# Mixer of a hybrid decoder trunk: products by V grouped by branch, weight splits queued behind a projection's first reader

## The chip, the cores and the metric

The kernel runs on one core of one Trainium2 chip, as one launch. The metric is the device time of that launch in microseconds (us), lower is better. A time of a kernel is the median of its runs; the profile is one further execution, with its own time.

## The reference, cut to what matters

Two layers, each of three sub-layers: a SwiGLU feed-forward block, a token mixer, a second feed-forward block. Sequence 256, width 1024, everything in float32. The change lies in the mixer alone:

```python
def _hybrid_mixer(u, w_in, b_gate, b_forget, w_branch, w_out):
    proj = u @ w_in
    a_qkv, b_qkv, i_q, i_k, i_w, c_qkv, d_qkv, f_logit, g_logit = jnp.split(proj, SPLIT_POINTS, axis=-1)
    ...                                     # A: 3 groups of 2 heads, dilated windows, rope, merged by softmax of lse
    y_b = _dsa_attention(qb, kb, vb, q_idx, k_idx, i_w).reshape(bsz, t, -1)      # 4 heads, rope, top 64 keys
    y_c = _stick_breaking_attention(qc, kc, vc).reshape(bsz, t, -1)              # 4 heads
    y_d = _forgetting_attention(qd, kd, vd, log_f).reshape(bsz, t, -1)           # 4 heads
    gates = jax.nn.sigmoid((g_logit + b_gate)...).reshape(bsz, t, N_BRANCH, D_MODEL)
    merged = gates[:, :, 0] * (y_a @ w_branch[...])
    for i in range(1, N_BRANCH):
        merged = merged + gates[:, :, i] * (branches[i] @ w_branch[...])
    return merged @ w_out
```

Every attention ends in a product of its weights p (256 x 256, causal) by V (256 x 64 a head).

## The kernel before

**Split products.** A product of float32 matrices runs as three matmuls on rounded halves: each operand is split into `hi` and `lo`, and `split_mm` (L289 to L295) adds hi by hi, hi by lo and lo by hi into a PSUM bank. The activations are split once per sub-layer (`uh`, `ul`). The weights are split as they arrive, in `load`: a DMA on SP's queue brings 128 x 1024 values into a `raw` tile (L261; five `raw` buffers, `RB`), ScalarE (ACT) rounds it to `hi` (L264), VectorE (DVE) subtracts to get `lo` (L270). A `raw` buffer is free for the next DMA when its `lo` is done. The reductions of the conditioning weights (L321, on DVE, from `adac`) take their `raw` buffers from the same five, in the same SP queue.

**Projections.** `proj` makes two blocks of 128 output channels into one PSUM bank from `mm_bank`, of which there are two. So projection n fills the bank that projection n-2 used, and waits until that one's readers are done. The readers are `rope` (DVE: L706 and L707 read the bank, then a shuffle, L708) for branches A, B and the indexer, and `plain` (ACT: L715) for C and D. The order in the program is: V of A (L1042), three projections of A (`qa`, `ka`), indexer `iq`, a `vproj` with the indexer's key, its weights and V of B and half of C, then `qb`, `kb`, `cq`, `ck`, a second `vproj` (V of C and D; its weights are 128 x 768 pieces, `mv`), `dq`, `dk`. Sixteen projections for the gates follow, with the branch products between them.

**Attention between the projections.** `plan` puts steps of the four attentions at numbered turns (`on`), which `tick` calls between projections. `a_scores`, `a_pt` and `a_pv` do branch A in two halves of 128 queries: scores, softmax (`soft`: minima on DVE L818, exponentials on ACT L820, reciprocal L821, scaling on ACT L824), transposes on TensorE (PE, L926) into a PSUM bank from `tp_bank`, of which there are two, a copy on ACT (L928) into a `pt` tile, products by V (L934). For C, D and B, `pair_pt` transposes two heads, `pair_pv` multiplies two heads by V (`pv`, L791 and L794) into a bank, and `y_out` rounds the 128 x 256 result to `yh` (ACT, L807) and `yl` (DVE, L808). Branch products (`tp<-y`) read these.

**What sets the order.** A scheduler orders each engine's instructions when the kernel is built, by program order and by priorities (`tc.high_priority(offset=...)` moves a block forward: `HP` for `load`, `RP` and `PP` for the readers, `VP` for V and y). Each engine then runs its list strictly in that order. `tc.issue_after(i)` puts what is traced inside it behind instruction i in that list, where both are on the same engine; it adds no wait between engines.

Of the kernel before, what the change touches and what calls it, by code (L numbers as in the profile page):

```python
# [18 lines left out]
D = 1024  # L19
# [44 lines left out]
GD = 3  # L64
PTB = 3
AST = 7
# [80 lines left out]
def trunk(ctx: ExitStack, tc: tile.TileContext, x, xT, crow, ada0, adac, adab, w_in0, w_in0x, gcol, bcol, ln_g, ln_b,  # L147
# [101 lines left out]

    def load(*srcs):  # L250

# [3 lines left out]
        for o in range(2):  # L255
            for src, n, half, got in zip(srcs, widths, halves, parts):
                if o * half >= n:
                    continue
                with tc.high_priority(offset=HP):
                    raw = wp.tile([P, 1024], F32, tag="raw", bufs=RB, name="raw")  # L260
                    nc.sync.dma_start(raw[:, :half], src[:, o * half:(o + 1) * half])  # L261
                    hi, lo = w_pair()
                    with behind() if held["free"] <= 0 < held["left"] else ExitStack():
                        nc.scalar.copy(hi[:, :half], raw[:, :half])  # L264
                        if held.get("pool_lo"):
                            held["pool_lo"] -= 1
                            nc.gpsimd.tensor_sub(lo[:, :half], raw[:, :half], hi[:, :half].bitcast(F32))
                        else:
                            with held["late"].pop(0) if held["late"] else ExitStack():
                                held["lo"] = nc.vector.tensor_sub(lo[:, :half], raw[:, :half], hi[:, :half].bitcast(F32)).ins  # L270
                    held["left"] -= 1
                    held["free"] -= 1
                    got.append((hi, lo))
# [394 lines left out]
    def mixer(l, u, nxt, steps):  # L668
# [15 lines left out]
        def tick():  # L684
            at["n"] += 1
            for f in turns.pop(at["n"], []):
                f()

        def proj(src, n):
            w = load(src.rearrange("p a b -> p (a b)"))  # L690
            ps = mm_bank()
# [9 lines left out]
        def rope(ps, name, scale=1.0):  # L701
# [3 lines left out]
            with tc.high_priority(offset=RP):  # L705
                nc.vector.scalar_tensor_tensor(t2, ps, scale, cs[:, C_SIN:C_SIN + 256], op0=ALU.mult, op1=ALU.mult)  # L706
                nc.vector.scalar_tensor_tensor(q, ps, scale, cs[:, C_COS:C_COS + 256], op0=ALU.mult, op1=ALU.mult)  # L707
            nc.vector.stream_shuffle(t3, t2, shuf)  # L708
            nc.gpsimd.tensor_tensor(q, q, t3, op=ALU.add)
            return q  # L710

        def plain(ps, scale, name):
            q = mp.tile([P, T], F32, tag="qk", bufs=QB, name=name)
            with tc.high_priority(offset=PP):
                nc.scalar.activation(q, ps, AF.Copy, scale=scale)  # L715
            return q

# [4 lines left out]
        def index_keys():  # L722
            ps = tp_bank()
            for t in range(2):
                nc.tensor.transpose(ps[:, t * 128:(t + 1) * 128], ik2[:, t].rearrange("p a b -> p (a b)"), ident)
            ik.append(rope(ps[:, :256], "ik"))

        wf = mp.tile([P, 2, 8], F32, tag="wf", bufs=1, name="wf")

        def vproj(srcs, width, piece, extra=0):  # L730
# [16 lines left out]
            else:  # L747
                for hf in range(2):
                    w = load(srcs[hf].rearrange("p a b -> p (a b)"))
                    for t in range(2):  # L750
# [46 lines left out]

        def y_out(y, k, t=None):

            c = slice(0, T) if t is None else slice(t * 128, t * 128 + 128)  # L800
            with tc.high_priority(offset=VP):
                if k in (0, 1, 3, 5) and not t:
                    ys["tile"] = alt([P, 4, T], F32R, "y")
                o = 2 * (k in (2, 4, 6))
                ys[k] = (ys["tile"][:, o], ys["tile"][:, o + 1])
                yh, yl = (z[:, c] for z in ys[k])
                nc.scalar.copy(yh, y)  # L807
# [83 lines left out]

        def pair_pv(br, j, k):
            y = acc_bank()
            pv(y, {h % 2: [(vh(br, h, 0), vh(br, h, 1), live.pop((br, h)))] for h in (2 * j, 2 * j + 1)})
            y_out(y[:, :T], k + j)

# [109 lines left out]
        def plan():  # L1006
# [15 lines left out]
            for j in range(2):  # L1022
                on(20 + CS + j, f(c_sums, j))
            for j in range(2):
                on(23 + CVV + j, f(pair_pv, "C", j, 3))
                on(26 + 6 * j, f(d_scores, j))
                on(38 + 6 * j, f(b_scores, j))
                on(29 + 6 * j, f(pair_pt, "D", j))
                on(30 + 6 * j, f(pair_pv, "D", j, 5))
                on(41 + 6 * j, f(pair_pt, "B", j))  # L1030
                on(42 + 6 * j, f(pair_pv, "B", j, 1))
            for n, t in enumerate(STEPS):
# [9 lines left out]
        vproj([mv12[l, 0, 0], mv12[l, 0, 1]], 384, 2)  # L1042
        qa, ka = [], []
        for i in range(3):
            for j, p in enumerate(proj(mpair[l, i], 2)):
                (qa if 2 * i + j < 3 else ka).append(rope(p, "qa", -0.125) if 2 * i + j < 3 else rope(p, "ka"))
        at["n"] = 0
        plan()
        iq = [rope(p, "iq") for p in proj(mpair[l, 3], 2)]
        vproj([mv0[l, 0], mv0[l, 1]], 456, 0, extra=72)  # L1050
        qb = [rope(p, "qb", -0.125) for p in proj(mpair[l, 4], 2)]
        kb = [rope(p, "kb") for p in proj(mpair[l, 5], 2)]
        cq = [plain(p, 0.125, "cq") for p in proj(mpair[l, 6], 2)]
        ck = [plain(p, 1.0, "ck") for p in proj(mpair[l, 7], 2)]
        vproj([mv12[l, 1, 0], mv12[l, 1, 1]], 384, 1)
        dq = [plain(p, -0.125, "dq") for p in proj(mpair[l, 8], 2)]
        dk = [plain(p, 1.0, "dk") for p in proj(mpair[l, 9], 2)]

# [166 lines left out]
```

## Time and profile before

| | |
|---|---|
| median of 3 runs | 1297.29 us (1295.61 to 1297.9) |
| the profiled execution | 1298.93 us, its span from first to last instruction 1297.1 us |
| PE busy | 1263.4 us, 97% |
| DVE busy | 1040.6 us, 80% |
| ACT busy | 655.5 us, 51% |
| granted PE clock, mean | 0.997 of full speed |
| mixers in the span | about 210 to 455 us and 850 to 1090 us |

The span is cut by what PE does, instruction after instruction. A matmul's own length in the timeline (0.28 us for 256 columns) is modelled and overlaps its neighbours; what it costs is the distance from its start to the next start, 0.12 us for 256 columns in a stream. So the places where PE waits show as wider steps between starts, with the releaser in brackets where one is known.

### The profile page before, as it was taken

Reading aid. Unit: us, or ns where it says so; the run is one execution under the profiler, and the core shown is the slowest. Engines: PE = TensorE matmul, PEld = TensorE weight load, DVE = VectorE, ACT = ScalarE, POOL = GpSimd, SP = SyncE. Lnnn points to the kernel's source line nnn. Section 1 sums busy time; section 2 is a strip of 40 time slices with the busy share of each in tenths; the row PEclk is TensorE's granted clock in tenths of the full one; section 3 lists DMA queues with packets and bytes.
Section 4 is the critical chain, followed back from the end, with each engine's and each line's share of the span. In section 5 each row is a group of like instructions: output and inputs, shape, how many; then the busy total and the mean of one; then the engine's idle time right before and its main releaser. Section 6 shows DMA issues by size and latency. Waiting matters only on the chain.

```text
span 1297.1 us, 23364 instructions
## 1 busy us (share of the span) xinstructions
PE 1263.4 (97%) x9178; PEld 1175.5 (91%) x9178; DVE 1040.6 (80%) x1701; ACT 655.5 (51%) x1023; POOL 144.6 (11%) x150
## 2 busy tenths in 40 slices
PE   6999999999999999999999999999999999999997
PEld 5989998999999889999989999898999997899995
DVE  7788987889796789986689976688989867896565
ACT  4563445447664465444364444454766554644440
POOL 0021000204131000000000000021071310000000
PEclk9999999999999999999999999999999999999999
DMA  9889963757775568975659875356577645765530
GB/s 341 332 280 361 375 241 131 240 177 235 241 253 195 206 235 309 327 256 191 211 191 316 322 255 179 118 184 216 195 245 248 236 168 199 275 236 185 194 132 33
DMA packets 85846, 300.41 MB, mean 232 GB/s; under 512 B 10604, under 2 KB 12316, under 8 KB 85736
## 3 DMA queue, kind: packets, MB, share of 16 engines
q1 hardware_dynamic: 84392, 298.00, 65.9%
q8 instruction: 72, 1.18, 0.3%
q10 hardware_dynamic: 576, 0.60, 0.1%
q0 software_dynamic: 768, 0.32, 0.1%
q14 instruction: 38, 0.31, 0.1%
HBM read 297.81 MB, written 1.07 MB: 230 GB/s over the span
## 4 chain that ended last, share of the span: by engine, by line
PE 76%; issue 8%; DVE 6%; DMA 5%; ACT 4%; POOL 1%; DVEq 0%; POOLq 0%; ACTq 0%; SPq 0%
PE mm L289 15%; PE mm L290 15%; PE mm L291 15%; PE acc L295 7%; PE acc L294 6%; PE acc L293 6%; ACT hi L264 2%; DVE lo L270 2%; PE tp L289 1%; DMA raw<-in_w_in_dram 1%; PE tp L290 1%; PE tp L291 1%; DMA raw<-in_w_out_dram 1%; DMA raw<-in_mpair_dram 1%; PE mm L293 1%
## 5 line engine op out<-in xcount | busy, mean ns | idle before, releaser
L270 DVE TENSOR_TENSOR lo<-raw,hi 128x1024 fp32r<-128x1024 f32 (+2 forms) x421 | 508.6, 1224 | 172.7 <-ACT hi L264 171.3
L264 ACT CAST hi<-raw 128x1024 fp32r<-128x1024 f32 (+1 forms) x422 | 434.7, 1041 | 367.4 <-PE mm L290 206.0
L289 PE MATMUL mm<-uh,hi 128*128 128x256 f32 x2032 | 574.4, 283 | 1.8 <-DVE qa L707 1.8
L290 PE MATMUL mm<-ul,hi 128*128 128x256 f32 x2032 | 571.3, 281 | 0.0
L291 PE MATMUL mm<-uh,lo 128*128 128x256 f32 x2032 | 570.5, 281 | 0.0
L289 PEld LDWEIGHTS mm<-uh,hi 128*128 128x128 f32 x2032 | 383.1, 189 | 8.2 <-issue 4.1
L290 PEld LDWEIGHTS mm<-ul,hi 128*128 128x128 f32 x2032 | 383.5, 189 | 1.4
L291 PEld LDWEIGHTS mm<-uh,lo 128*128 128x128 f32 x2032 | 383.3, 189 | 0.3
L295 PE MATMUL acc<-hi,hl 128*128 128x512 f32 x352 | 138.3, 398 | 4.0 <-DVE hl L558 3.8
L293 PE MATMUL acc<-hi,hh 128*128 128x512 f32 x352 | 140.2, 398 | 0.4 <-ACT hh L557 0.4
L294 PE MATMUL acc<-lo,hh 128*128 128x512 f32 x352 | 139.0, 395 | 0.0
L321 DVE CUSTOM_DVE_ANT_0 adac<-adac,cond_row,adab 128x1024 f32<-128x1024 f32 x80 | 101.8, 1284 | 3.0 <-DMA adac<-in_adac_dram 3.0
L295 PEld LDWEIGHTS acc<-hi,hl 128*128 128x128 f32 x352 | 65.7, 187 | 22.6 <-DVE hl L558 6.6
L293 PEld LDWEIGHTS acc<-hi,hh 128*128 128x128 f32 x352 | 66.1, 188 | 15.1 <-ACT hh L557 1.2
L294 PEld LDWEIGHTS acc<-lo,hh 128*128 128x128 f32 x352 | 66.1, 188 | 13.8
L557 ACT CAST hh<-h 128x256 fp32r<-128x256 f32 x82 | 33.2, 405 | 82.1 <-DVE h L551 82.1
L321 DVE CUSTOM_DVE_ANT_0 raw<-raw,cond_row,adab 128x1024 f32<-128x1024 f32 x48 | 66.9, 1408 | 0.0
L434 POOL TENSOR_TENSOR rstd<-rstd,nhalf 128x1 f32<-128x1 f32 x12 | 7.6, 634 | 475.1 <-DVE rstd L433 475.1
L558 DVE TENSOR_TENSOR hl<-h,hh 128x256 fp32r<-128x256 f32 x74 | 31.3, 423 | 12.6 <-ACT hh L557 12.6
L1102 POOL TENSOR_TENSOR merged<-merged,tg 128x512 f32<-128x512 f32 x16 | 28.0, 1752 | 120.2 <-DVE tg L1100 57.7
L293 PE MATMUL acc<-hi,uh 128*128 128x256 f32 (+1 forms) x128 | 38.8, 303 | 0.8 <-ACT uh L462 0.8
L295 PE MATMUL acc<-hi,ul 128*128 128x256 f32 (+1 forms) x128 | 38.1, 298 | 0.0
(243 smaller groups left out, 1551.7 us busy)
## 6 DMA issues: line engine op xcount, KB each, us to landing
raw<-in_w_in_dram SPq DMA_DIRECT2D x174, 512.0 KB, 5.5
raw<-in_mpair_dram SPq DMA_DIRECT2D x104, 512.0 KB, 4.7
raw<-in_w_out_dram SPq DMA_DIRECT2D x88, 512.0 KB, 5.2
adac<-in_adac_dram SPq DMA_DIRECT2D x80, 512.0 KB, 6.9
raw<-in_adac_dram SPq DMA_DIRECT2D x48, 512.0 KB, 4.5
ada<-in_ada_dram SPq DMA_DIRECT2D x16, 512.0 KB, 6.7
raw<-in_mwo_dram SPq DMA_DIRECT2D x16, 512.0 KB, 4.4
raw<-in_mv_dram SPq DMA_DIRECT2D x16, 384.0 KB, 3.6
```

What stands on the lines that cost most here:

```text
L264: nc.scalar.copy(hi[:, :half], raw[:, :half])
L270: held["lo"] = nc.vector.tensor_sub(lo[:, :half], raw[:, :half], hi[:, :half].bitcast(F32)).ins
L289: nc.tensor.matmul(ps, lhsT=wh, rhs=xh, start=start, stop=False)
L290: nc.tensor.matmul(ps, lhsT=wh, rhs=xl, start=False, stop=False)
L291: nc.tensor.matmul(ps, lhsT=wl, rhs=xh, start=False, stop=stop)
L293: nc.tensor.matmul(ps, lhsT=xh, rhs=wh, start=start, stop=False)
L294: nc.tensor.matmul(ps, lhsT=xh, rhs=wl, start=False, stop=False)
L295: return nc.tensor.matmul(ps, lhsT=xl, rhs=wh, start=False, stop=stop).ins
L321: nc.vector.tensor_tensor_reduce(raw, raw, cond_row, 0.5, adab_sb[:, l * 3 + s, v, n:n + 1], ALU.mult, ALU.add, accum_out=t[:, n:n + 1])
L557: nc.scalar.copy(hh, h)
L558: eng.tensor_sub(hl, h, hh.bitcast(F32))
L1102: eng.tensor_tensor(mg, mg, t, op=ALU.add)
```

## The change

Three things change, all in the mixer.

1. `pair_pv` (two heads) becomes `branch_pv` (four heads): both pairs' products by V go into the two halves of one PSUM bank, and one ACT copy and one DVE subtraction of 512 columns make `yh` and `yl` of the whole branch. It is called at one turn per branch (28 for C, 36 for D, 48 for B) where `pair_pv` was called at 27 and 28, 30 and 36, 42 and 48. `PTB`, the number of `pt` buffers, goes from 3 to 4.
2. `load` takes a list `after`; the split of the weights (L264, L270) is queued behind these instructions. `proj` and the `vproj` passes give it `readers[-2:-1]`: the first reader (L707, or L715 where the projection is `plain`) of the projection two back, the one whose bank they wait for.
3. Readers are recorded by `pair`, and forgotten after each `vproj`.

```diff
-PTB = 3
+PTB = 4
@@ load
-    def load(*srcs):
+    def load(*srcs, after=()):
...
-                    with behind() if held["free"] <= 0 < held["left"] else ExitStack():
+                    with behind() if held["free"] <= 0 < held["left"] else ExitStack() as order:
+                        for i in after:
+                            order.enter_context(tc.issue_after(i))
                         nc.scalar.copy(hi[:, :half], raw[:, :half])
@@ mixer
+        readers = []
         def proj(src, n):
-            w = load(src.rearrange("p a b -> p (a b)"))
+            w = load(src.rearrange("p a b -> p (a b)"), after=readers[-2:-1])
...
@@ vproj
-                    w = load(srcs[hf].rearrange("p a b -> p (a b)"))
+                    w = load(srcs[hf].rearrange("p a b -> p (a b)"), after=readers[-2:-1])
@@ y_out: A alone, a tile of its own
-                if k in (0, 1, 3, 5) and not t:
-                    ys["tile"] = alt([P, 4, T], F32R, "y")
+                if t == 0:
+                    ys["tile"] = alt([P, 2, T], F32R, "y")
@@
-        def pair_pv(br, j, k):
+        def branch_pv(br, k):
             y = acc_bank()
-            pv(y, {h % 2: [(vh(br, h, 0), vh(br, h, 1), live.pop((br, h)))] for h in (2 * j, 2 * j + 1)})
-            y_out(y[:, :T], k + j)
+            for j in range(2):
+                pv(y[:, j * T:(j + 1) * T], {h % 2: [(vh(br, h, 0), vh(br, h, 1), live.pop((br, h)))] for h in (2 * j, 2 * j + 1)})
+            with tc.high_priority(offset=VP):
+                both = alt([P, 2, 2, T], F32R, "y")
+                for j in range(2):
+                    ys[k + j] = (both[:, 0, j], both[:, 1, j])
+                yh, yl = (both[:, n].rearrange("p a b -> p (a b)") for n in range(2))
+                nc.scalar.copy(yh, y)
+            nc.vector.tensor_sub(yl, y, yh.bitcast(F32))
@@ plan
+            on(24 + CVV, f(branch_pv, "C", 3))
+            on(36, f(branch_pv, "D", 5))
+            on(48, f(branch_pv, "B", 1))
             for j in range(2):
-                on(23 + CVV + j, f(pair_pv, "C", j, 3))
...
-                on(30 + 6 * j, f(pair_pv, "D", j, 5))
...
-                on(42 + 6 * j, f(pair_pv, "B", j, 1))
@@ the projections
+        def pair(i, *makes):
+            got = [make(p) for make, p in zip(makes, proj(mpair[l, i], 2))]
+            readers.append(got[0][1])
+            return [q for q, _ in got]
...
+        qka = pair(0, aq, aq) + pair(1, aq, ak) + pair(2, ak, ak)
...
+        iq = pair(3, *[roped("iq")] * 2)
         vproj([mv0[l, 0], mv0[l, 1]], 456, 0, extra=72)
+        readers.clear()
+        qb = pair(4, *[roped("qb", -0.125)] * 2)
+        kb = pair(5, *[roped("kb")] * 2)
+        cq = pair(6, *[copied("cq", 0.125)] * 2)
+        ck = pair(7, *[copied("ck", 1.0)] * 2)
         vproj([mv12[l, 1, 0], mv12[l, 1, 1]], 384, 1)
+        readers.clear()
```

The changed kernel's line numbers run ahead: L264 of before is L266, L270 L272, L706 and L707 L712 and L713, L708 L714, L715 L721, L820 L825, L824 L829, L852 L857, L928 L941, L791 and L794 L797 and L800. Outside the two mixers, the order on every engine is as it was; SP's order of DMAs is the same throughout.

The first projections of A, on DVE (`lo` is a weight's split, `mm` the bank of a projection). Before:

```order
L270 TENSOR_TENSOR lo<-raw,hi 128x1024 x7
L706 SCALAR_TENSOR_TENSOR t_2485<-mm,cs 128x256
L707 SCALAR_TENSOR_TENSOR qa<-mm,cs 128x256
L270 TENSOR_TENSOR lo<-raw,hi 128x1024
L708 STREAM_SHUFFLE t_2486<-t_2485 128x256
L706 SCALAR_TENSOR_TENSOR t_2492<-mm,cs 128x256
L707 SCALAR_TENSOR_TENSOR qa<-mm,cs 128x256
```

Now, the same place:

```order
L272 TENSOR_TENSOR lo<-raw,hi 128x1024 x4
L712 SCALAR_TENSOR_TENSOR t_2485<-mm,cs 128x256
L713 SCALAR_TENSOR_TENSOR qa<-mm,cs 128x256
L272 TENSOR_TENSOR lo<-raw,hi 128x1024 x2
L714 STREAM_SHUFFLE t_2486<-t_2485 128x256
L712 SCALAR_TENSOR_TENSOR t_2492<-mm,cs 128x256
L713 SCALAR_TENSOR_TENSOR qa<-mm,cs 128x256
```

Three splits that stood ahead of the first reader of the first bank stand behind it, and the later ones follow the later readers.

The second half of branch A, on ACT (`pa` is A's softmax, `cq` and `ck` are copies of projections, `rel` the indexer's scores, `hi` of 128x768 the weights of the second `vproj`, `hi` of 128x1024 those of `dq`). Before; the four copies `pt<-tp` (L928) come next:

```order
L264 CAST hi<-raw 128x768 x2
L852 ACTIVATE rel<-acc 128x384 x2
L264 CAST hi<-raw 128x768
L820 ACTIVATE pa,su<-pa,mn 128x768
L715 ACTIVATE cq<-mm 128x256 x2
L264 CAST hi<-raw 128x768
L820 ACTIVATE pa,su<-pa,mn 128x768
L852 ACTIVATE rel<-acc 128x384
L824 ACTIVATE pa<-pa,su 128x768 x2
L852 ACTIVATE rel<-acc 128x384
L264 CAST hi<-raw 128x1024 x2
L715 ACTIVATE ck<-mm 128x256 x2
```

Now, the same place, down to the `pt` copies:

```order
L857 ACTIVATE rel<-acc 128x384 x2
L825 ACTIVATE pa,su<-pa,mn 128x768 x2
L829 ACTIVATE pa<-pa,su 128x768
L721 ACTIVATE cq<-mm 128x256 x2
L266 CAST hi<-raw 128x768 x3
L829 ACTIVATE pa<-pa,su 128x768
L857 ACTIVATE rel<-acc 128x384 x2
L266 CAST hi<-raw 128x768
L721 ACTIVATE ck<-mm 128x256 x2
L266 CAST hi<-raw 128x1024
L941 COPY pt<-tp 128x384 x2
L266 CAST hi<-raw 128x1024
```

All four casts of 768 columns stand behind the copies of `cq`, where three stood ahead of them; the casts of 1024 columns stand just ahead of the `pt` copies as before, and one of them between these.

The products by V of branch C, on PE (`zm` are C's weights). Before, the first pair; the second comes 24 matmuls of a gate later:

```order
L291 MATMUL tp<-y,lo 128x256
L791 MATMUL acc<-zm,V 64x256 x2
L794 MATMUL acc<-zm,V 64x128 x2
L289 MATMUL mm<-uh,hi 128x256
L290 MATMUL mm<-ul,hi 128x256
```

Now:

```order
L293 MATMUL mm<-uh,lo 128x256
L797 MATMUL acc<-zm,V 64x256 x2
L800 MATMUL acc<-zm,V 64x128 x2
L797 MATMUL acc<-zm,V 64x256 x2
L800 MATMUL acc<-zm,V 64x128 x2
L291 MATMUL mm<-uh,hi 128x256
```

C's two groups are one. Those of D and B stay two in PE's order: the first now follows the second pair's transposes, the second stays behind the branch product that follows these.

## Rows read from the trace of the kernel before

**Rows 1.** Who PE waited for, whole span: total us, times, longest.

```profile
PE mm L289 <- DVE qa L707: 1.8, 2, 1.4
```

**Rows 2.** Timeline of PE at projections' waits: start us, us, instruction [idle<-releaser].

```profile
225.48 0.28 PE L291 MATMUL mm<-uh,lo 128*128 128x256 f32 x1
227.17 0.36 PE L289 MATMUL mm<-uh,hi 128*128 128x256 f32 x1 [1.41 <-DVE qa L707]
...
243.58 0.47 PE L293 MATMUL mm<-hi,uh 128*128 128x456 f32 x1 [0.23 <-DVE iq L707]
...
864.43 0.36 PE L289 MATMUL mm<-uh,hi 128*128 128x256 f32 x1 [0.39 <-DVE qa L707]
```

**Rows 3.** Timeline of DVE ahead of the first of these waits.

```profile
223.00 1.23 DVE L270 TENSOR_TENSOR lo<-raw,hi 128x1024 fp32r<-128x1024 f32 x1 [3.01 <-ACT hi L264]
224.14 0.42 DVE L706 SCALAR_TENSOR_TENSOR t<-mm,cs 128x256 f32<-128x256 f32 x1
```

**Rows 4.** Timeline of PE around the first products by V of C.

```profile
320.44 0.28 PE L291 MATMUL tp<-y,lo 128*128 128x256 f32 x1
320.65 0.65 PE L791 MATMUL acc<-zm,V 128*64 128x256 f32 x4
...
321.45 0.39 PE L289 MATMUL mm<-uh,hi 128*128 128x256 f32 x1
321.68 0.28 PE L290 MATMUL mm<-ul,hi 128*128 128x256 f32 x1
```

**Rows 5.** Timeline of DVE, then PE: B's y done, and its first reader.

```profile
387.19 0.41 DVE L808 TENSOR_TENSOR y<-acc,y 128x256 fp32r<-128x256 f32 x1
...
416.70 0.28 PE L289 MATMUL tp<-y,hi 128*128 128x256 f32 x1
```

**Rows 6.** Timeline of PE: scores of A's second half, its second transposes.

```profile
267.52 1.57 PE L904 MATMUL acc<-ka,qa 64*128 64x256 f32 x12
...
280.74 0.34 PE L294 MATMUL mm<-lo,uh 128*128 128x384 f32 x1
281.11 0.93 PE L926 MATMUL tp<-ident,pa 128*128 128x128 f32 x6
```

**Rows 7.** Timeline of DVE in the same stretch: first minimum, a split of 768 columns.

```profile
270.88 0.68 DVE L818 CUSTOM_DVE_ANT_0 pa<-acc,ms 128x512 f32<-128x512 f32 x1
...
274.94 0.96 DVE L270 TENSOR_TENSOR lo<-raw,hi 128x768 fp32r<-128x768 f32 x1 [1.09 <-ACT hi L264]
```

**Rows 8.** Timeline of ACT in the same stretch.

```profile
272.62 0.94 ACT L820 ACTIVATE pa<-pa,mn 128x768 f32<-128x768 f32 x1 [1.15 <-DVE mn L818]
...
273.55 0.64 ACT L715 ACTIVATE cq<-mm 128x256 f32<-128x256 f32 x2
274.08 0.83 ACT L264 CAST hi<-raw 128x768 fp32r<-128x768 f32 x1
274.80 0.95 ACT L820 ACTIVATE pa<-pa,mn 128x768 f32<-128x768 f32 x1
...
276.11 1.76 ACT L824 ACTIVATE pa<-pa,su 128x768 f32<-128x768 f32 x2
...
280.01 0.68 ACT L715 ACTIVATE ck<-mm 128x256 f32<-128x256 f32 x2
280.56 0.88 ACT L928 COPY pt<-tp 128x384 f32<-128x384 f32 x2
```

**Rows 9.** Timeline of SP's queue: DMA issues of the weights of `dq`.

```profile
265.59 4.51 SPq L261 DMA_DIRECT2D raw<-in_mpair_dram  x2
```

**Rows 10.** DMA view, second mixer, 900 to 905 us: KB each, us from issue to landing.

```profile
raw<-in_mpair_dram SPq DMA_DIRECT2D x1, 512.0 KB, 4.4
raw<-in_mv_dram SPq DMA_DIRECT2D x1, 384.0 KB, 3.0
```

**Rows 11.** The page's DMA issues, whole span: KB each, median us to landing.

```profile
raw<-in_w_in_dram SPq DMA_DIRECT2D x174, 512.0 KB, 5.5
```

**Rows 12.** Timeline of ACT: A's first half, the copies of its transposes.

```profile
253.45 0.86 ACT L928 COPY pt<-tp 128x384 f32<-128x384 f32 x2 [1.30 <-PE tp L926]
```

More of the change, by code (lines that the diff above doesn't have):

```diff
@@ L706, in rope @@
                 nc.vector.scalar_tensor_tensor(t2, ps, scale, cs[:, C_SIN:C_SIN + 256], op0=ALU.mult, op1=ALU.mult)
-                nc.vector.scalar_tensor_tensor(q, ps, scale, cs[:, C_COS:C_COS + 256], op0=ALU.mult, op1=ALU.mult)
+                last = nc.vector.scalar_tensor_tensor(q, ps, scale, cs[:, C_COS:C_COS + 256], op0=ALU.mult, op1=ALU.mult).ins
             nc.vector.stream_shuffle(t3, t2, shuf)
             nc.gpsimd.tensor_tensor(q, q, t3, op=ALU.add)
-            return q
+            return q, last
         def plain(ps, scale, name):
@@ L714, in plain @@
             with tc.high_priority(offset=PP):
-                nc.scalar.activation(q, ps, AF.Copy, scale=scale)
-            return q
+                last = nc.scalar.activation(q, ps, AF.Copy, scale=scale).ins
+            return q, last
         V = {}
@@ L725, in index_keys @@
                 nc.tensor.transpose(ps[:, t * 128:(t + 1) * 128], ik2[:, t].rearrange("p a b -> p (a b)"), ident)
-            ik.append(rope(ps[:, :256], "ik"))
+            ik.append(rope(ps[:, :256], "ik")[0])
         wf = mp.tile([P, 2, 8], F32, tag="wf", bufs=1, name="wf")
@@ L796, in mixer, with y_out @@
         ys = {}
-        def y_out(y, k, t=None):
-            c = slice(0, T) if t is None else slice(t * 128, t * 128 + 128)
+        def y_out(y, k, t):
+            c = slice(t * 128, t * 128 + 128)
             with tc.high_priority(offset=VP):
-                if k in (0, 1, 3, 5) and not t:
-                    ys["tile"] = alt([P, 4, T], F32R, "y")
-                o = 2 * (k in (2, 4, 6))
-                ys[k] = (ys["tile"][:, o], ys["tile"][:, o + 1])
+                if t == 0:
+                    ys["tile"] = alt([P, 2, T], F32R, "y")
+                ys[k] = (ys["tile"][:, 0], ys["tile"][:, 1])
                 yh, yl = (z[:, c] for z in ys[k])
@@ L1042, in mixer @@
         vproj([mv12[l, 0, 0], mv12[l, 0, 1]], 384, 2)
[L1043 to L1046, printed above, removed]
+        def pair(i, *makes):
+            got = [make(p) for make, p in zip(makes, proj(mpair[l, i], 2))]
+            readers.append(got[0][1])
+            return [q for q, _ in got]
+        roped = lambda name, scale=1.0: lambda p: rope(p, name, scale)
+        copied = lambda name, scale: lambda p: plain(p, scale, name)
+        aq, ak = roped("qa", -0.125), roped("ka")
+        qka = pair(0, aq, aq) + pair(1, aq, ak) + pair(2, ak, ak)
+        qa, ka = qka[:3], qka[3:]
         at["n"] = 0
         plan()
-        iq = [rope(p, "iq") for p in proj(mpair[l, 3], 2)]
+        iq = pair(3, *[roped("iq")] * 2)
         vproj([mv0[l, 0], mv0[l, 1]], 456, 0, extra=72)
[L1051 to L1054, printed above, removed]
+        readers.clear()
[3 more added lines that the diff above has]
+        ck = pair(7, *[copied("ck", 1.0)] * 2)
         vproj([mv12[l, 1, 0], mv12[l, 1, 1]], 384, 1)
-        dq = [plain(p, -0.125, "dq") for p in proj(mpair[l, 8], 2)]
-        dk = [plain(p, 1.0, "dk") for p in proj(mpair[l, 9], 2)]
+        readers.clear()
+        dq = pair(8, *[copied("dq", -0.125)] * 2)
+        dk = pair(9, *[copied("dk", 1.0)] * 2)
+        readers.clear()
         merged = mp.tile([P, KT, T], F32, tag="big8", bufs=3, name="merged")
```

## The prediction

> **What bounds the kernel now.** I read the table of busy times first: PE is busy for 97% of the span, so what PE does not wait for costs nothing, and a change that leaves PE's matmuls as they are can move only PE's waits. Next the view of who PE waited for. In the mixers it has one entry of weight, the third and fifth projections' bank, which `qa`'s readers on DVE still held [rows 1]. The timeline of PE shows these waits at their places [rows 2]; the reader is to look at the distance between starts, not at the bracket alone. From 225.48 to 227.17 are 1.69 us where a step takes 0.12, so this wait cost 1.57, which is 0.16 more than its bracket. With the same 0.16 the other three cost 0.39 (243.58), 0.55 (864.43) and 0.39 (a row like that of 243.58 stands in the second mixer at 880.84). DVE explains the first [rows 3]: PE had filled the bank two projections earlier, one projection being 48 matmuls or some 5.7 us, so at about 219.9, but L706 read it only at 224.14, since it stood behind a split that itself waited 3.01 us for ACT.
>
> Last I read the places where PE does not wait before but stands close to its supplier. The closest is branch A's second half [rows 6 to 8]: PE's second group of transposes starts at 281.11, the end of the first `pt` copy is at about 281.04, and that copy frees the bank. There is no slack at all.
>
> **The change part by part.**
>
> *Readers ahead of splits.* In DVE's new order three splits no longer stand ahead of the first reader. Then L706 and L707 run at about 220, two splits (2.3 us) and the second block's readers (0.8 us, after a shuffle of 0.4) follow, and the bank is free at about 224.3, before PE asks at 225.6. `iq`'s two readers now stand together too. I count all four waits as gone: 1.57 + 0.39 + 0.55 + 0.39 = **2.9 us gained**. If only the brackets go, it is 1.41 + 0.23 + 0.39 + 0.23 = 2.3.
>
> *Products by V.* A group of them costs PE more than its matmuls at both ends [rows 4]: it starts 0.21 after the last matmul where 0.12 is a step, and the second matmul behind it comes 0.23 after the first. That is 0.09 + 0.11 = 0.2 us for a group. C's two groups become one: 0.2 a mixer. D and B keep two groups in PE's order; the first moves from behind a branch product to behind transposes, a joint that the trace does not show. It gives between nothing and another 0.2 each. So 0.2 to 0.6 a mixer; I take 0.3, nearest to what is shown, **0.6 us gained** in two mixers (0.4 to 1.2).
>
> *One y of 512 columns instead of two of 256.* It takes three copies off ACT and three subtractions off DVE a mixer, and makes the first pair's y later. Neither is on PE's path: B's y is done at 387.19 and first read at 416.70 [rows 5], and C and D are read as they were, some 30 us and 20 us behind theirs. I cost it at nothing; it would cost only if y came more than 20 us later.
>
> *Splits behind `cq`.* This is the edit that costs. The weights of the second `vproj` (four pieces of 768 columns) now wait in ACT's list for the copy of `cq`, which stands behind A's exponentials. Before, three were cast ahead of them and `dq`'s weights were issued at 265.59 [rows 9]. Five `raw` buffers are the reason that a late cast is a late DMA: a piece goes out when the split five loads earlier is done. In the changed kernel's clock, where PE is 1.57 + 0.39 = 1.96 us ahead of the old one here, the chain is:
>
> - A's scores end at 267.52 + 1.57 - 1.96 = 267.1; DVE's minima begin at 267.2 (the reductions that stood ahead of them now stand behind).
> - The first exponential 1.74 us later (270.88 to 272.62 [rows 7, 8]) at 268.9, the second 0.93 later at 269.9, the first scaling 1.31 after that (274.80 to 276.11) at 271.2, done with at 272.0.
> - `cq`'s two copies 0.53; the casts at 272.55, 273.3 and 274.0 (0.72 apart, 274.08 to 274.80).
> - The first split: cast done 273.4, subtraction 0.96, so 274.4, and SP issues the last `mv` piece. The second is done at 275.3, and SP issues `dq`'s first weights, ten us later than before.
> - `mv` lands after 3.0 us (277.4), is cast until 278.1, `ck`'s copies (0.55 from 280.01 to 280.56) end at 278.7. `dq`'s weights land after 4.4 us [rows 10], at 279.7. That pair of DMAs, one `mv` and then one `mpair`, is the same as here. The cast of 1024 columns (1.04) ends at 280.8, and only behind it comes the `pt` copy (0.48), done at 281.3.
> - PE would ask for that bank at 280.74 + 0.17 - 1.96 = 278.95, and starts at 281.35: a **new wait of 2.4 us a mixer, 4.8 in two**.
>
> The bounds: with any landing under 3.3 us ACT itself is the limit, at 278.7 + 0.95 + 0.48 = 280.1, a wait of 1.2; with 5.5 us, the page's median for 512 KB in long bursts [rows 11], it is 3.5. So 2.4 to 7.0 in two mixers. I take 4.8, since rows 10 are the nearest case. The Trainium skill, "DMA: Bandwidth & Descriptors", Anatomy of one DMA, gives about 2.0 us plus bytes at 436 GB/s, for GpSimd's queue, which is an estimate of 3.2 us for 512 KB. By it the wait would be 1.2 a mixer, and the sum below would be -0.5 in place of +1.9. The rows for this queue do not agree (4.4 and 5.5), and I go by them.
>
> *The same in A's first half.* There, too, two casts stand just ahead of the `pt` copies, and their DMAs come later, since two reductions that free `raw` buffers moved behind splits. ACT was idle for 1.30 us ahead of these copies [rows 12], which hides most of it. What is left falls on the transposes of the indexer's key (L725), which need the same bank. No row shows its size: nothing if the idle time holds it, at most about as much again, 1.3. I take 0.3, near the lower end, **0.6 in two mixers** (0 to 2.6).
>
> The sum: -2.9 - 0.6 + 4.8 + 0.6 = **+1.9 us**. Against the profiled execution's span of 1297.1 that is 1299.0, and 1300.8 for that execution's 1298.93. It lay 1.6 above the median of the runs; on the median, 1297.29, the forecast is **1299.2 us**, 0.15% more. The ends: -2.9 - 1.2 + 2.4 + 0 = -1.7, and -2.3 - 0.4 + 7.0 + 2.6 = +6.9.
>
> **The rivals.** A difference of 0.2%, 2.6 us, is about what a measurement of this kernel can tell from none.
>
> *Faster.* The `pt` copies are in time in A's second half, because the casts ahead of them find their weights landed. For it: PE's order puts these transposes where they were, and DVE and ACT are less crowded there without the reductions. Against it: the order on ACT allows no other way round the cast. Then -2.9 - 0.6 + 0.6 = -2.9: 1294.4. It decides where the new waits stay under 0.9 us in all.
>
> *Slower.* The late weights come in a burst and land as bursts do, and the wait at A's transposes is the 3.5 us of the upper end, with 1.3 in the first half: -2.9 - 0.6 + 7.0 + 2.6 = +6.1, 1303.4. For it: four DMAs are issued there within 4 us once the buffers are free. It is slower than 0.2% from 6.1 us of new waits on, 3.05 a mixer, where I forecast 2.7.
>
> *It does not do what it says.* The order behind a reader binds on the reader's engine alone, so for roped projections ACT's casts go on as before, and the readers on DVE might still be late. Then the gain is missing: -0.6 + 4.8 + 0.6 = +4.8, 1302.1. DVE's order speaks against it.
>
> **How the numbers follow.** No change within 0.2%: 0.54, for the sum with its wait between 1 and 3 us a mixer. Faster: 0.14. Slower: 0.32, of which 0.28 for the burst and 0.04 for the missing gain. The time is that of the first, 1299.2. The range leaves out the ends of the two others: 1294.4 to 1303.0.
>
> **What would show it.** In PE's waits, `qa L707` and `iq L707` go to nothing; L926 gets an entry released by ACT's `pt` L941, twice, of 1.2 to 3.5 us, and L725 twice a small one. ACT shows a cast of 1024 columns released by a DMA just ahead of the second half's `pt` copies, and SP issues `dq`'s weights about ten us later than before. C's products by V stand as one group of eight. I am wrong if L926 does not wait, if the waits on `qa` stay, or if the branch products wait for y.

## The result and the profile after

| | before | after |
|---|---|---|
| median of the runs | 1297.60 us (1295.61 to 1298.26) | 1315.51 us (1313.91 to 1317.14) |
| ratio, 95% interval | | 1.0145 (1.013 to 1.016) |
| profiled execution's span | 1297.1 us | 1313.7 us |
| granted PE clock, mean | 0.997 | 0.991 |

The change costs 1.45%, some 18 us, where 1.9 us (0.15%) were forecast. Who PE waited for, whole span of the changed kernel (total us, times, longest):

```profile
PE tp L291 <- ACT uh L363: 12.4, 1, 12.4
PE tp L939 <- ACT pt L941: 8.0, 2, 4.1
PE tp L731 <- ACT pt L941: 5.2, 2, 2.9
PE tp L291 <- ACT pt L788: 3.5, 2, 2.2
...
PE mm L291 <- ACT V L765: 1.9, 2, 1.1
```

The first row is the start of the kernel and was there before. The entry of [rows 1], the readers of `qa`, is gone, and so are the other waits of [rows 2]. In their place stand four kinds of waits, all for ACT, of which the prediction had two; of the four, only that for L788 stood there before, once, with 0.3 us. L939 is L926 of before (branch A's transposes), L731 is L725 (the indexer's key), L765 the copy of V out of a projection's bank, L788 the `pt` copies of B, C and D ahead of a branch product.

Where the time went is seen best stretch by stretch. A mixer is taken here from the first transposes ahead of it (L452 before, L454 after) to the first transposes behind it:

```profile
200.24 0.38 PE L454 MATMUL mm<-ident,x 128*128 128x128 f32 x2
...
465.98 0.44 PE L454 MATMUL mm<-ident,x 128*128 128x128 f32 x2 [1.25 <-ACT x L444]
...
848.00 0.38 PE L454 MATMUL mm<-ident,x 128*128 128x128 f32 x2
...
1112.11 0.44 PE L454 MATMUL mm<-ident,x 128*128 128x128 f32 x2 [1.41 <-ACT x L444]
```

So the mixers took 265.7 and 264.1 us. The same rows of before:

```profile
200.55 0.38 PE L452 MATMUL mm<-ident,x 128*128 128x128 f32 x2
...
455.70 0.44 PE L452 MATMUL mm<-ident,x 128*128 128x128 f32 x2 [1.47 <-ACT x L442]
...
838.84 0.38 PE L452 MATMUL mm<-ident,x 128*128 128x128 f32 x2
...
1093.44 0.44 PE L452 MATMUL mm<-ident,x 128*128 128x128 f32 x2 [2.20 <-ACT x L442]
```

They took 255.2 and 254.6 there. The two mixers lost 20.1 us. The rest, whose instructions stand in the same order, was 3.5 us shorter in this pair of executions.

Inside a mixer I compared the start of PE's n-th product with that of before, both counted from the mixer's start. The difference moves in these steps (first mixer; second):

| step | us |
|---|---|
| the readers' waits gone | -1.9; -0.8 |
| the bank of V (L765), new | +1.3; +0.9 |
| L731, and the products behind it | +3.9; +4.4 |
| L939, and what stands behind it | +6.2; +4.8 |
| from C's products by V to B's branch product | +1.3; +1.1 |

The third and fourth step are more than their waits (2.4 and 2.9; 4.1 and 3.9). The granted clock tells why. Busy time of PE, then granted clock, DMA share and GB/s of the changed kernel, by stretches:

```profile
224.00:228.00 4.00, 4.00 (x36) 1.00 0.47 166
252.00:256.00 4.00, 1.63 (x15) 1.00 0.91 338
256.00:260.00 4.00, 4.00 (x24) 0.57 0.26 105
284.00:288.00 4.00, 0.18 (x2) 0.89 0.96 342
288.00:294.00 6.00, 5.71 (x36) 0.51 0.90 320
294.00:298.00 4.00, 4.00 (x29) 1.00 0.16 65
```

Behind the two long waits PE runs for about 3 and 5.5 us at 1.2 GHz in place of 2.4. The timeline shows the same: behind L731, products of 256 columns follow each other every 0.21 us where 0.12 is a step.

```profile
256.51 0.42 PE L291 MATMUL mm<-uh,hi 128*128 128x256 f32 x1
256.72 0.42 PE L292 MATMUL mm<-ul,hi 128*128 128x256 f32 x1
```

A second count agrees: PE's busy time in the two mixers, for the same products, rises from 501.2 to 506.5 us, so some 5 of the 20.1 us are slower products and the rest is idle time. The trace of before has one such stretch too, directly behind its second mixer, where PE had waited 2.20 us for `x`:

```profile
1093.40:1097.40 4.00, 3.96 (x15) 0.57 0.00 0
```

Now the chain of the second half, which the prediction had worked out. SP's issues, then ACT, in the first mixer of the changed kernel:

```profile
280.10 0.33 SPq L261 DMA_DIRECT2D raw<-in_mv_dram  x1
280.98 0.97 SPq L261 DMA_DIRECT2D raw<-in_mpair_dram  x1
```

```profile
277.73 0.63 ACT L721 ACTIVATE cq<-mm 128x256 f32<-128x256 f32 x2
278.26 2.30 ACT L266 CAST hi<-raw 128x768 fp32r<-128x768 f32 x3
...
283.45 0.84 ACT L266 CAST hi<-raw 128x768 fp32r<-128x768 f32 x1 [1.30 <-DMA raw<-in_mv_dram]
284.19 0.65 ACT L721 ACTIVATE ck<-mm 128x256 f32<-128x256 f32 x2
286.82 1.04 ACT L266 CAST hi<-raw 128x1024 fp32r<-128x1024 f32 x1 [1.98 <-DMA raw<-in_mpair_dram]
287.77 0.85 ACT L941 COPY pt<-tp 128x384 f32<-128x384 f32 x2
```

And PE, which waits for the first of these two copies:

```profile
283.85 0.34 PE L296 MATMUL mm<-lo,uh 128*128 128x384 f32 x1
288.30 1.54 PE L939 MATMUL tp<-ident,pa 128*128 128x128 f32 x6 [4.11 <-ACT pt L941]
```

Three casts directly behind `cq`, a cast of 1024 columns that waits for its weights, and only then the `pt` copies: link for link the chain of the forecast, and `dq`'s weights go out 15 us later than in [rows 9] (the whole kernel is 3 us later there).

The first half was not worked out, and it is where most of the error lies. DVE and ACT of the changed kernel:

```profile
231.85 4.16 DVE L272 TENSOR_TENSOR lo<-raw,hi 128x912 fp32r<-128x912 f32 x4
```

```profile
240.27 1.05 ACT L266 CAST hi<-raw 128x1024 fp32r<-128x1024 f32 x1 [8.25 <-DMA raw<-in_mpair_dram]
...
246.41 1.05 ACT L266 CAST hi<-raw 128x1024 fp32r<-128x1024 f32 x1 [2.57 <-DMA raw<-in_mpair_dram]
247.38 0.62 ACT L825 ACTIVATE pa<-pa,mn 128x384 f32<-128x384 f32 x1
...
248.80 0.48 ACT L765 COPY V<-mm 128x384 f32<-128x384 f32 x1
...
253.00 1.04 ACT L266 CAST hi<-raw 128x1024 fp32r<-128x1024 f32 x1 [2.09 <-DMA raw<-in_mpair_dram]
254.23 1.04 ACT L266 CAST hi<-raw 128x1024 fp32r<-128x1024 f32 x1 [0.19 <-DMA raw<-in_mpair_dram]
255.18 0.85 ACT L941 COPY pt<-tp 128x384 f32<-128x384 f32 x2
```

The four splits of the first `vproj`'s weights (912 columns) stand together behind a reader of `ka`, at 231.85; before, they ran at 227.28, 228.96, 232.57 and 234.27, between the readers. So their `raw` buffers come free late, and SP issues the next four weights from 234.00 on where it was 230.09 (the second row is of before):

```profile
234.00 8.93 SPq L261 DMA_DIRECT2D raw<-in_mpair_dram  x4
```

```profile
230.09 8.17 SPq L261 DMA_DIRECT2D raw<-in_mpair_dram  x4
```

ACT, idle for 8.25 us, then meets late weights three times: A's exponentials and the copy of V stand behind the fourth of these casts, the `pt` copies that L731 waits for behind the fifth and sixth. DVE is late with the same weights. A's minima, which the exponentials need, begin there at 246.79, behind the split of the third cast, and the first is done at 247.35, so the exponentials could not have begun sooner without the fourth cast either.

### The profile page after: what moved, and what is told of

It reads as the page before. It is cut to its first block, busy times and chain, and to the rows that moved or that the text cites. A ratio compares the mean times of both kernels' runs of the same rounds, so it can differ in the third digit from the quotient of the medians.

```text
span 1313.7 us, 23330 instructions
## 1 busy us (share of the span) xinstructions
PE 1266.9 (96%) x9178; PEld 1179.5 (90%) x9178; DVE 1040.5 (79%) x1695; ACT 652.9 (50%) x1017; POOL 138.7 (11%) x150
## 4 chain that ended last, share of the span: by engine, by line
PE 73%; issue 8%; DMA 7%; DVE 6%; ACT 5%; POOL 0%; DVEq 0%; SPq 0%; ACTq 0%; POOLq 0%
PE mm L291 15%; PE mm L293 15%; PE mm L292 15%; PE acc L297 7%; PE acc L295 7%; PE acc L296 7%; DMA raw<-in_mpair_dram 3%; DVE lo L272 3%; ACT hi L266 2%; DMA raw<-in_mbr_dram 1%; DMA raw<-in_w_out_dram 1%; PE tp L291 1%; PE tp L292 1%; PE tp L293 1%; DVE raw L323 1%
## 5 line engine op out<-in xcount | busy, mean ns | idle before, releaser
L272 DVE TENSOR_TENSOR lo<-raw,hi 128x1024 fp32r<-128x1024 f32 (+2 forms) x421 | 508.4, 1225 | 160.5 <-ACT hi L266 157.2
L266 ACT CAST hi<-raw 128x1024 fp32r<-128x1024 f32 (+1 forms) x422 | 434.3, 1041 | 382.4 <-PE mm L292 190.7
```

## The experiments

Ratios are to the kernel before, run beside each on the same chip, with 95% intervals. Every kernel computes everything, except that e7 adds work that nobody reads.

**1. The grouping alone, and the order alone.**

```diff
-            w = load(src.rearrange("p a b -> p (a b)"), after=readers[-2:-1])
+            w = load(src.rearrange("p a b -> p (a b)"))
```

(e1; the same in `vproj`. e2 keeps these lines and puts `pair_pv`, its turns and `PTB = 3` back.)

> The grouping of the products by V alone; no split is queued behind a reader. Theory 1 (the grouping is worth what the prediction said, and all of the loss is the splits' order): ratio 0.9995, 0.6 us faster, the four waits on the readers of qa and iq stay, and no wait of the transposes on ACT's pt copies over 0.5 us. Theory 2 (the late y or the fourth pt buffer makes the new waits of 2.2 and 1.3 us behind the pt copies at L788): those two waits stay, and the time is 3 us over the kernel before, ratio 1.0025.

> The splits behind the readers alone; products by V in pairs and three pt buffers, as in the kernel before. Theory 1: the whole loss and 0.6 us more, some 1316 us, ratio 1.014 to 1.015. Theory 2 (the grouping has its share in the waits behind L788): 1312, ratio 1.011.

Measured: e1 1.0018 (1.0007 to 1.0029), e2 1.0148 (1.0135 to 1.0161). The order has the whole loss. The grouping's own cost is not settled by the ratios: e1 stands 0.18% above the kernel before, the changed kernel 0.03% below e2. The waits behind L788 are the grouping's, as theory 2 had it: 1.2 and 0.8 us in e1, none in e2. But e1's mixers took 254.4 and 254.7 us, no more than before: in its first mixer the wait on `qa` is gone, although the order of every engine and of SP's DMAs is that of before up to 320 us. There the split ahead of the reader waited 1.20 us where [rows 3] has 3.01:

```profile
221.82 1.23 DVE L272 TENSOR_TENSOR lo<-raw,hi 128x1024 fp32r<-128x1024 f32 x1 [1.20 <-ACT hi L266]
222.96 0.41 DVE L712 SCALAR_TENSOR_TENSOR t<-mm,cs 128x256 f32<-128x256 f32 x1
```

So the wait of 1.57, more than half of the gain that was forecast, is not there in every execution. By the n-th product the grouping's stretch costs 0.35 and 0.17 us a mixer. The profiled execution lost its 3.3 us elsewhere, in the feed-forward block behind the first mixer (195.7 us for 191.1), where PE ran at half clock twice, behind waits of 1.8 and 1.9 us; it is the slowest of e1's 12 executions (1295.4 to 1302.2).

**2. Which binding.** e3 frees the second `vproj`'s weights, e4 the first's:

```diff
-        vproj([mv12[l, 1, 0], mv12[l, 1, 1]], 384, 1)
+        readers.clear(); vproj([mv12[l, 1, 0], mv12[l, 1, 1]], 384, 1)
```

```diff
-                    w = load(srcs[hf].rearrange("p a b -> p (a b)"), after=readers[-2:-1])
+                    w = load(srcs[hf].rearrange("p a b -> p (a b)"), after=readers[-2:-1] if piece else ())
```

> The changed kernel, but the weights of the second vproj (the 768-column pieces) are not queued behind the copy of cq. Theory 1 (each vproj's binding makes the waits of its own half): L939's two waits of 4.3 and 4.1 us go, and with them the lower clock behind them (4.5 us); L731 and L291 on V stay: 1303 us, ratio 1.0045. Theory 2 (the second half is late as an echo of the first, whose DMAs went out late): L939 still waits 3 us or more a mixer, 1311 us or more.

> The changed kernel, but the weights of the first vproj behind the indexer (the 912-column pieces) are not queued behind the reader of ka. Theory 1: the waits of the first half go (L291 on V, 1.3 and 0.9; L731, 2.5 and 3.0) with the lower clock behind them (3.4 us); L939 stays with 4 us a mixer: 1305 us, ratio 1.0055. Theory 2 (echo): L939's waits fall too, to the 2.4 us of the prediction or less, 1300 us or under.

Measured: e3 1.0063 (1.0043 to 1.0083), e4 1.0090 (1.0077 to 1.0103). In e3 no wait at L939 is left; in e4 L939 waits as long as in the changed kernel while L765 is gone and L731 is down to 0.8:

```profile
PE tp L939 <- ACT pt L941: 7.8, 2, 4.1
...
PE tp L731 <- ACT pt L941: 0.8, 1, 0.8
```

So each binding makes the waits of its own half, and the second half is no echo of the first. By the ratios they are worth 0.82% and 0.55%, some 10.6 and 7.1 us of the 18.8, each known to about 3.

**3. Neither `vproj` bound.** e5 binds the projections' own splits alone, with pairs of products by V (the expectation counts the projections from 0); e8 does so with the grouping.

> The splits of the second, third, sixth and seventh projection of the mixer queued behind readers as in the change; those of both vprojs not; products by V in pairs, as in the kernel before. Theory 1 (all of the loss is in the two vprojs' bindings, and the readers run earlier as the prediction had it): the waits on qa and iq go, L731 and L939 (here L932) wait at most 0.3, and the time is 1 to 3 us below the kernel before: ratio 0.998 to 0.9995. Theory 2 (any binding on DVE holds raw buffers back and makes the first half late): L731 or L291 on V wait 1 us or more a mixer, ratio 1.002 or more.

> The changed kernel without the bindings of the two vprojs. Theory 1 (the parts add up): the ratio of the projections' binding alone plus 0.0018 for the grouping of the products by V, some 1.001, with the waits behind the pt copies at L788 of about 1 us a mixer that the grouping alone had too. Theory 2 (the two removed bindings do not add up, something else of the change is left): 1.004 or more.

Measured: e5 1.0013 (1.0004 to 1.0022), e8 1.0007 (0.9998 to 1.0016). The two bindings have the whole loss, and the grouping (e8 against e5) adds nothing that could be measured. But e5 is not faster than before: the waits on `qa` and `iq` go, and PE waits at the next projection for the reader of `ka` instead (0.57 in both mixers) and for the `pt` copies at L731 (0.55 and 0.82):

```profile
PE mm L291 <- DVE ka L713: 1.1, 2, 0.6
```

A split that no longer stands ahead of one reader stands ahead of the next.

**4. What of L939's wait is the cast that waits.** e6 lets ACT's `pt` copies go ahead of that cast:

```diff
-                nc.scalar.copy(pt, ps[:, :384])
+                with tc.high_priority(offset=400): nc.scalar.copy(pt, ps[:, :384])
```

> The changed kernel with ACT's copies of branch A's transposes (L941) given a priority 400 higher, so that in the second half they stand ahead of the cast of 1024 columns that waits for the late DMA; the first half's order stays. Theory 1 (what holds PE at L939 is that cast, whose weights land late): the waits of 4.3 and 4.1 us at L939 fall under 0.5, the lower clock behind them goes: 1304 us, ratio 1.006. Theory 2 (exponentials, scaling and the three 768-column casts are late by themselves): L939 still waits 2 us or more, 1309 us or more, ratio 1.010.

Measured: 1.0112 (1.0096 to 1.0128); L939 still waits 2.4 and 2.1 us. Both theories in part: the cast of 1024 columns and its idle time make some 1.8 us; the rest is the last cast of 768 columns and `ck` behind it, which also wait for a late DMA (ACT of e6):

```profile
281.84 0.83 ACT L266 CAST hi<-raw 128x768 fp32r<-128x768 f32 x1 [1.70 <-DMA raw<-in_mv_dram]
282.57 0.65 ACT L721 ACTIVATE ck<-mm 128x256 f32<-128x256 f32 x2
283.11 0.86 ACT L941 COPY pt<-tp 128x384 f32<-128x384 f32 x2
```

Not all of the 4 us between the two ratios need be the cast's. In the first mixer e6's profile is already 3.2 us ahead of the changed kernel's at A's first products by V, with the same order up to there: PE waited 0.5 us for V in place of 1.1 and 1.3 at L731 in place of 2.4, and the clock behind it stayed full. Single executions differ by that much.

**5. The clock.** e7 fills the wait with products that nobody reads:

```diff
+            live["Ay"] = acc_bank()
             for i in range(0, len(blocks), 3):
+                for n in range(48 if i == 6 else 0):
+                    nc.tensor.matmul(live["Ay"][:, 256:512], lhsT=ones, rhs=uh[:, n % KT], start=True, stop=True)
...
-            blocks, y = a_blocks(t), acc_bank()
+            blocks, y = a_blocks(t), live["Ay"]
```

> The changed kernel with 48 matmuls of 256 columns that nobody reads (5.7 us at 0.119 each) ahead of the transposes of branch A's second half that wait, on PE, twice; PE's order puts the 12 matmuls that stood between the two groups of transposes behind them, so the stretch to fill is 6.2 us. Theory 1 (the granted clock falls because PE stood idle, and that costs 4.5 us in the two second halves): the clock stays 1.00 there and the time is 4 us below the changed kernel, 1311.5, ratio 1.011. Theory 2 (the clock falls with something else, the burst of DMAs say): it still falls to 0.5, and the time is that of the changed kernel or above, ratio 1.0145 or more.

Measured: 1.0179 (1.0161 to 1.0198). The clock part of theory 1 holds. These are e7's filling, its stretches, then the products by V behind the wait in e7 and in the changed kernel (the kernel before took 1.93 us for these 24 at full clock):

```profile
280.23 5.88 PE L938 MATMUL acc<-uh,cr 128*128 128x256 f32 x48
```

```profile
280.00:286.00 6.00, 6.00 (x54) 1.00 0.91 277
286.00:290.00 4.00, 4.00 (x41) 1.00 0.92 345
```

```profile
288.80 1.53 PE L950 MATMUL acc<-pt,V 128*64 128x128 f32 x24
```

```profile
291.05 2.83 PE L947 MATMUL acc<-pt,V 128*64 128x128 f32 x24
```

With PE busy the clock stays at 2.4 GHz under the same load of DMAs (0.92 here, 0.90 in 288 to 294 above), in both mixers; e7's one stretch at half clock in a mixer is behind L731 of the second, a wait of 3.4 us that was not filled. In before's row above the clock was down with the DMA share at 0.00. So it falls with PE's idling and not with the transfers. The time part fails: the kernel is no faster. The filling took 5.9 us where the wait was 4.1, the moved products by V gave a new wait for y's subtraction on DVE (1.4 and 0.5 us, at C's scores), and PE's order had changed; how these add up to the ratio is not shown. What the clock costs in the total is therefore taken from the steps above, not from this run.

**6. The number of `raw` buffers.** Six in place of five, with 13 `qk` buffers to make room: e10 (control, five), e9 (six everywhere) and e13 (a sixth for the mixers' weights alone), each on the order alone; e11 and e12 the same two on the kernel before.

```diff
-RB, QB = 5, 15
+RB, QB = 6, 13
```

> The splits behind readers alone (pairs of products by V, as in the run of the order alone), with 13 qk buffers in place of 15: the control for the next one. Both theories: as the order alone, ratio 1.0148, L932 waits 4.5 to 4.9 us and L731 2.5 to 3.2 us a mixer.

> The same with six raw buffers in place of five (13 qk buffers make the room). Theory 1 (a late split becomes a late DMA because only five raw buffers stand between them, and PE waits for what these DMAs bring late): every DMA goes out one split earlier, L932's waits fall under 2.5 us and L731's under 1, ratio 1.005 to 1.008. Theory 2 (the waits come from the order on ACT and DVE itself, whenever the weights land): L932 still waits 4 us a mixer, ratio 1.012 or more.

> The kernel before with six raw and 13 qk buffers. Theory 1 (its own waits on the readers of qa come from a split that waited 3.0 us for its weights ahead of the reader, so an earlier DMA shortens them): the wait of 1.57 falls under 0.8, ratio 0.998 to 1.000. Theory 2 (two qk buffers fewer cost more than the raw buffer gives): a new wait in the mixers and a ratio of 1.001 or more.

> The kernel before with a sixth raw buffer that only the mixer's weights use (every sixth load), and 13 qk buffers; in the feed-forward blocks it loads through five as before. In the run with six raw buffers everywhere the mixers took 251.6 us each in place of 255.2 and 254.6, and the feed-forward blocks 8 us more. Theory 1 (the gain belongs to the mixers' own DMAs, the loss to the feed-forward blocks' order): mixers 251 to 252 us each, the rest as before, 6 us less in all, ratio 0.995. Theory 2 (the 13 qk buffers cost the feed-forward blocks their time, whatever raw does): the mixers gain but the rest loses, ratio 1.000 or more.

> The splits behind readers alone, with the same sixth raw buffer for the mixer's weights. Theory 1 (a late split makes a late DMA through the count of raw buffers): with one more the waits behind pt copies (L731, L932) and on V fall from 11 us of the control with five to 6 or less over both mixers, and the mixers together from 527.8 us to 519 or less. Theory 2 (the waits are the order's): mixers together 525 us or more. With six everywhere they took 518.4, but there the feed-forward blocks' order had moved as well.

Measured: e10 1.0170 (1.015 to 1.019), e9 1.0181 (1.0161 to 1.0201), e13 1.0092 (1.0073 to 1.0111), e11 1.0061 (1.004 to 1.0082), e12 0.9992 (0.9981 to 1.0003). Mixers: e10 263.8 and 264.1 us, e9 259.1 and 259.3, e13 259.4 and 259.7, e11 251.6 and 251.6, e12 252.0 and 251.6. One more buffer takes 8.7 us from the bound mixers (e13 against e10), the time that theory 1 named, but not by the waits that it named. Those behind `pt` copies and on V fall from 14.0 us in e10 (the expectation has 11) to 8.9, not to 6: L731's to 0.9 at most and V's to none, while L932's stay at 3.5 and 3.7. In the first half two others come in, 1.8 (L932, for ACT's scaling of `pa`) and 1.7 (a product that waits for `iq`'s reader). PE's busy time in the two mixers, on the same products, falls by 5.1 of the 8.7 us (508.3 to 503.2), which is the clock: e10 drops to half behind all four waits at L731 and L932, e13 behind the two at L932 alone. In e9 the waits are those that theory 1 forecast for it, none at L731 and 2.3 and 2.5 at L932, beside new ones for `iq`'s reader and `pa` (6.3 in all), and its mixers are as short as e13's; its ratio, 1.005 to 1.008 by theory 1, did not follow. So the count of buffers bears on the waits of both halves. How far the order does is not shown: the scheduler moved part of it on PE, ACT and DVE in e9 and e13.

In the totals, 13 `qk` buffers lengthen the very end (from the last mixer's end 201.7 us in e2, 205.8 in e10), and six `raw` buffers everywhere cost e11's feed-forward blocks some 9 us against e12, with waits for their hidden values on DVE (3.2 at L551, 2.1 at L558). So e12's mixers gain 6.2 us and the interval of its ratio holds 1.

**7. The readers' waits without any reordering.** On the kernel before, two (e14) or four (e15) early loads of a mixer land in an idle big tile, so that the DMAs behind them go out earlier:

```diff
-                    raw = wp.tile([P, 1024], F32, tag="raw", bufs=RB, name="raw")
+                    held["n"] = held.get("n", 0) + held.get("early", 0); six = held.get("early") and held["n"] in (5, 11); raw = mp.tile([P, 2048], F32, tag="big8", bufs=3, name="raw6")[:, :1024] if six else wp.tile([P, 1024], F32, tag="raw", bufs=RB, name="raw")
...
```

> The kernel before; two of the mixer's early loads (the fifth and eleventh behind V of A) go into a big tile that stands idle there (big8), so that the DMAs behind them go out one raw buffer earlier. No order on PE, ACT or DVE changes. Theory 1 (the wait of 1.57 on qa is a late DMA ahead of a split ahead of the reader): the wait on qa goes, the mixers take 252 to 253.5 us each in place of 255.2 and 254.6, ratio 0.997 to 0.999. Theory 2 (the DMA engines, busy for 0.8 of the time there, are the limit and an earlier issue lands no earlier): waits and time as before, ratio 1.000.

> The same with four such loads (5, 8, 11, 14). Theory 1: the wait on iq falls too; mixers 251.5 to 252.5 us each, ratio 0.996 to 0.998. Theory 2: as before, 1.000.

Measured: 0.9994 (0.998 to 1.0009) and 0.9992 (0.9978 to 1.0007). The wait on `qa` is gone in both mixers, and the n-th product is 1.65 and 0.6 us earlier from there to the mixer's end. DVE of e14, where [rows 3] had a split that waited 3.01 us for its weights:

```profile
213.70 8.22 DVE L270 TENSOR_TENSOR lo<-raw,hi 128x1024 fp32r<-128x1024 f32 x7 [0.53 <-ACT hi L264]
221.84 0.42 DVE L706 SCALAR_TENSOR_TENSOR t<-mm,cs 128x256 f32<-128x256 f32 x1
```

The same seven splits stand ahead of the reader, and it is in time. The reader was late for want of weights, not for its place in the list. e15's two further loads gave nothing: the waits on `iq` stay (0.4 us in all), and its mixers take 253.4 and 254.5 us, e14's 253.4 and 253.1. Faster than before by 0.06 to 0.08% by the middle of the intervals, which hold 1: none of the versions tried is shown to beat the kernel before.

## Why the prediction was wrong, point by point

- **What bounds, and the readers' gain: right for the profiled execution.** The waits of [rows 1, 2] are gone. 2.9 us were forecast, and the n-th product shows 1.9 + 0.8 = 2.7. The entry of [rows 1] is the third projection of either mixer, not a third and a fifth. e1 shows that its larger part comes and goes with the execution, so the gain was priced from one execution that had it in full.
- **Splits behind `cq`: the right chain, 2.4 us a mixer for 4.3 and 4.1.** From the end of A's scores (272.34) the casts start 5.92 us later (forecast 5.45): the minima stood behind two of the indexer's sums, 0.57 in place of 0.1. SP issues the last `mv` and `dq`'s first weights 1.84 and 2.72 us after the casts began (forecast 1.85 and 2.75). Then the cast of these weights starts 5.84 us behind their issue, where a landing of 4.4 was taken from [rows 10]; this term alone is 1.44 us. 0.47 + 1.44, and 0.05 less on what follows, make the difference. The upper end of 3.5 went by the median of [rows 11], a landing of 5.5, and was too low as well. The estimate of 3.2 from the Trainium skill ("DMA: Bandwidth & Descriptors", Anatomy of one DMA) was further off still: for this queue, with another weight and two conditioning weights issued before these had landed, the rows decide.
- **A's first half: the step that failed most.** I costed it at 0.3 a mixer, at most 1.3, by the idle time of [rows 12]; it cost 10.5 in two mixers with the clock behind it. Measured: L731 2.4 and 2.9, and a wait on V's bank of 1.3 and 0.9 that the prediction didn't have. I followed the second `vproj`'s weights through ACT, DVE and SP, and not the first's, which are bound in the same line of the change. e4 and e5 put the cause there. That it works through the `raw` buffers is what the rows of SP, DVE and ACT above say; e13 agrees for L731 and V, but its order had moved too.
- **The clock: not in the sum at all.** The steps behind L731 and L939 exceed their waits by some 1.5 us at L731 (both mixers) and by 2.1 and 0.9 at L939, together some 6 us. In the kernel before, whose longest wait in a mixer is 1.57 us, the mixers show no such stretch, but the row at 1093.40 does, behind a wait of 2.20: the trace at hand showed it for a wait about as long as the forecast one. The Trainium skill, "TensorE: Matmul & The Clock Gate", HAM oscillation, says that waits for the next operand's DMA between bursts of matmuls bring the array back to its lower clock and that the burst behind starts at it. The rows above agree (0.57 and 0.51), with ACT's copies in place of the DMA.
- **The grouping: -0.6 forecast, +0.5 measured** in e1 (0.35 and 0.17). The saved starts are there (one group less a mixer), but B's second `pt` copies now stand just ahead of B's branch product, which waits up to 1.2 us for the bank; 2.2 and 1.3 in the changed kernel. The prediction looked for a wait for y there and put that at nothing; it had no term for this bank.
- **The rivals.** The slower one had the right sign and place and ended at 1303.4; it let the wait grow and had 1.3 a mixer for the first half, too little there, and nothing for the clock. The third rival did not happen: the readers are early.

The sum by measured terms, two mixers: -2.7 + 2.2 (V) + 8.3 (L731 with its clock) + 11.0 (L939 with its clock) + 2.4 (grouping's stretch) - 0.1 (small shifts) = +21.1 at the mixers' last products. The spans say +20.1, since the transposes behind them waited 1.0 us longer for `x` in the execution of before (1.47 and 2.20, now 1.25 and 1.41).

What stays open: how the 20.1 divides between idle and clock to better than 1 us, since each step is read from one execution of each kernel; and how much of the readers' 2.7 us an ordinary execution of the kernel before has to give. The profiled one was 1.6 us above the median, e1 lacks 1.4 of them with no change there, and e14, which has them gone, gained less than could be measured.

## What to carry to other kernels

When an order is bound at one call that serves several loads, follow every load that it binds through all its queues, not only the one that looks worst: a split that waits holds its buffer, the buffer holds the next DMA, and in a list that runs strictly in order the late weights then hold everything behind their cast. Before moving work away from ahead of a late reader, ask why the reader is late: here an earlier DMA removed the same wait with no order changed. And look in the trace at hand for what the clock does behind PE's longest waits before pricing a new one: behind the four long waits of the changed kernel the half clock added between a quarter and two thirds of the wait.

## What the runs showed of the hardware that I had not expected

- PE's clock after a wait: waits of 2.4, 2.9, 3.9 and 4.1 us of the changed kernel were each followed by about 3 to 5.5 us at half clock, e7's two filled ones by none. But it is not the length of the wait alone: 2.4 us at L939 of e6, 2.4 at L731 in e2's second mixer and 2.8 behind e15's second mixer were followed by a full clock, while 1.8 behind e1's first mixer and 1.6 in a feed-forward block of e8 (at 1119 us) were followed by half of it.
- `dq`'s first weights, 512 KB, took 4.3 and 4.4 us to land in the two mixers of before, and 5.8 and 5.6 at the same places of the changed kernel. In both they were issued behind one 384 KB transfer; before, no other was issued for 4 us behind them, while in the changed kernel another weight and two conditioning weights were, within 4.4 us, and the share of DMA in use was 0.96 (284 to 288 us).
